# Attention in larger steps: eight transposes at once, value products of 256 queries in two steps beside the sums' reciprocals in one bank

## The chip, the cores and the metric

The kernel runs on one core of a Trainium2 chip. A core has a matrix engine (TensorE, "PE" in the profile; its weight loads are listed apart as "PEld"), a vector engine (VectorE, "DVE"), a scalar engine (ScalarE, "ACT"), a general engine (GpSimd, "POOL") and an engine that issues most transfers (SyncE, "SP"). Each works through its own queue in order, and semaphores tie the queues together. PE writes to PSUM alone, which has eight banks of 128 partitions by 512 float32 numbers; ScalarE and VectorE read them from there.

The metric is the device time of one execution in microseconds, less is better. A measurement is a median over some runs.

## The reference

The model is an encoder trunk of two layers, with 1024 tokens of width 1024 in float32. Layer 0 mixes tokens in two ways side by side: attention with 8 query heads and 2 key heads of width 64, and an RWKV-7 scan of 8 heads in both directions. Layer 1 mixes them with long filters (Hyena). Each layer ends with a SwiGLU network. The change lies in the attention of layer 0 alone:

```python
def one_block(q_blk):
    s = jnp.einsum('bqhgd,bkhd->bhgqk', q_blk, k, preferred_element_type=jnp.float32) * scale
    p = jax.nn.softmax(s, axis=-1)
    return jnp.einsum('bhgqk,bkhd->bqhgd', p.astype(v.dtype), v)
```

Queries go in blocks of 128 against all 1024 keys. The queries and keys were normed and rotated by then.

## The kernel before

**The stage.** `mixer` first streams the input projection (with the first unit's preparation beside it), and then works on the RWKV scan in eight units, one for each pair of heads (`hp`) and direction (`d`). In the loop at the end of `mixer`, turn `i` weaves together what is left of unit `i - 2` (`rwkv_s`: the recurrence over 16 chunks of tokens, one after the other, each a product on PE, then a multiply and add on VectorE at L1500), the products of unit `i - 1` (`rwkv_y`) and the preparation of unit `i` (`rwkv_x`, which ends with a block matrix W that is written to DRAM and read back in another order; L1374 is the first product that needs it). The fourth thread of the weave, `other`, is attention: `beside` goes through `attention` step by step, and when it is through, through `hy_filters`, which prepares the Hyena filters. `weave` takes from its generators in proportion to the steps that each is said to have; a `yield` in a generator is the place where it gives way. The tuple at L1615 says how many steps `other` gets in each turn. The numbers in `beside` (L1607) say after which of attention's steps a piece of the filters' hidden layer is slipped in. The order made so is the program's order; a scheduler that simulates the engines then settles each engine's queue and may move an instruction ahead of others that it takes to be still waiting.

**Attention.** It has 64 score steps: four pairs of heads `t`, eight query blocks `qt`, two heads `e` of the pair. For each,

- `scores` makes 128 queries x 1024 keys in two PSUM banks (L952 and L953, two halves of 512 keys), the maximum of each row on VectorE (L956, L957) and the exponential on ScalarE (L960), which also adds up the row's sum. The result is a page `pr` in SBUF.
- `turn` works on the step before. It turns the 128 x 1024 probabilities over, so that the keys lie on partitions: PE transposes blocks of 128 x 128 (L975, a product with the identity), four into a bank, and ScalarE copies the bank to SBUF (L976). It gives way after each four.
- `values`, after each second query block, multiplies the turned probabilities of 256 queries with the values, for both heads (L996; a float32 product of this kind appears as two matmul records). It gives way after every second of the eight key blocks. Its output stands in the bank `o`, which is taken at `qt` 1 or 5 and kept over two calls until it holds 512 queries. Then the row sums are added up and inverted on VectorE (L1003, L1004), PE spreads them over 64 partitions per head into another bank `rb` (L1008), ScalarE copies them to SBUF (L1010), and VectorE multiplies them with `o` (L1011).

Attention has the four banks of group 1 (`set_banks(4, 4)`), the scan the other four. `bank` takes the bank that has been free longest in the program's order, and `fbank` puts it back at the end of the row; an instruction that reuses a bank waits for the last reader of it.

**Forms of matmul.** The profile names the part of PE's array that a matmul uses. Scores and transposes use 128\*128, value products and the reciprocals' products 128\*64, most products of the scan 64\*64 (L1374, L1430, L1440, L1457, L1499), its preparation 64\*128 (L1310), and a few of its steps 128\*64 (L1421, L1482, L1514) or 128\*128 (L1392).

Of the kernel before, what the change touches and what calls it, by code (L numbers as in the profile page):

```python
# [13 lines left out]
ALU = mybir.AluOpType  # L14
# [7 lines left out]
P = 128  # L22
# [6 lines left out]
H64 = (slice(0, 64), slice(64, 128))  # L29
# [17 lines left out]
def weave(*gens):  # L47


    live = [[0, n, g] for n, g in gens]  # L50
    while live:
        live.sort(key=lambda x: x[0] / x[1])
        s = live[0]
        try:
            cost = next(s[2])
            if cost != "wait":
                s[0] += cost or 1
            elif len(live) > 1:
                s[0] = s[1] * (live[1][0] / live[1][1] + 1e-6)
        except StopIteration:  # L60
            live.pop(0)
# [7 lines left out]
def some(gen, n):  # L69

    for _ in range(n):
        if next(gen, gen) is gen:
            return
        yield


class Kern:
# [834 lines left out]
    def attention(self, out, G):  # L912

        nc = self.nc
        st = {}

        def keys(g):

            kn = self.unspill(self.qd["k"], nc.gpsimd)
            kh, kl = self.page(dt=F32R), self.page(dt=F32R)  # L920
            for X in (g, 1 - g):
                nc.scalar.activation(out=kh[H64[X]], in_=kn[H64[g]], func=AF.Copy)
            for X in (g, 1 - g):
                nc.vector.tensor_tensor(out=kl[H64[X]], in0=kn[H64[g]], in1=kh[H64[g]].bitcast(F32), op=ALU.subtract)
            self.free(kn)
            return kh, kl

        def queries(t):

            q = self.unspill(self.qd[t], nc.gpsimd)  # L930
            qs = [self.page(dt=F32R) for _ in range(2)]
            for e in range(2):
                nc.scalar.activation(out=qs[e][H64[e]], in_=q[H64[e]], func=AF.Copy)
                nc.vector.tensor_tensor(out=qs[e][H64[1 - e]], in0=q[H64[e]], in1=qs[e][H64[e]].bitcast(F32), op=ALU.subtract)
            self.free(q)
            return qs

        def scores(t, qt, e):

            if qt == 0 and e == 0:  # L940
                if t % 2 == 0:
                    if t:
                        self.free(st["k"])
                    st["k"] = keys(t // 2)
                st["qs"] = queries(t)
            if qt % 4 == 0 and e == 0:
                st["s", qt // 4] = self.small("sums", [P, 4, 2, 2], 3)
            kh, kl = st["k"]
            q = st["qs"][e][:, qt * P : (qt + 1) * P]
            ps = [self.bank(G) for _ in range(2)]  # L950
            for n in range(2):
                nc.tensor.matmul(ps[n], q, kh[:, HALVES[n]], start=True, stop=False)  # L952
                nc.tensor.matmul(ps[n], q, kl[:, HALVES[n]], start=False, stop=True)  # L953
            m = self.small("mx", [P, 4], 4)
            for n in range(2):
                nc.vector.tensor_reduce(out=m[:, n : n + 1], in_=ps[n], axis=AX.X, op=ALU.max)  # L956
            nc.vector.tensor_scalar(out=m[:, 2:3], in0=m[:, 0:1], scalar1=m[:, 1:2], scalar2=-0.125, op0=ALU.max, op1=ALU.mult)  # L957
            pr = self.page()
            for n in range(2):
                nc.scalar.activation(out=pr[:, HALVES[n]], in_=ps[n], func=AF.Exp, scale=0.125, bias=m[:, 2:3],  # L960
                                     accum_out=st["s", qt // 4][:, qt % 4, e, n : n + 1])
            self.fbank(ps)
            if qt == 7 and e == 1:
                self.free(st["qs"])
            return pr

        def turn(pr, t, qt, e):

            if qt % 2 == 0:
                st["p", e] = [self.page((P, 4, 256)) for _ in range(2)]  # L970
            for n in range(2):
                pt = self.bank(G, (P, 4, P))
                for j in range(4):
                    k = 4 * n + j
                    nc.tensor.transpose(pt[:, j], pr[:, k * P : (k + 1) * P], self.ident)  # L975
                nc.scalar.copy(st["p", e][n][:, :, P * (qt % 2) : P * (qt % 2) + P], pt)  # L976
                self.fbank(pt)
                yield
            self.free(pr)

        def values(t, qt):

            if "v" not in st:
                st["v"] = self.page((P, 8, P))
                nc.gpsimd.dma_start(out=st["v"].rearrange("p a b -> p (a b)"), in_=self.vd)
            v = st["v"]
            if qt == 1:
                st["y"] = self.page()
            if qt % 4 == 1:
                st["o"] = self.bank(G)  # L990
            o, g = st["o"], t // 2
            x = (qt % 4 - 1) * P
            pT = [st.pop(("p", e)) for e in range(2)]
            for k in range(8):
                for e in range(2):
                    nc.tensor.matmul(o[H64[e], x : x + 256], v[:, k, H64[g]], pT[e][k // 4][:, k % 4], start=k == 0, stop=k == 7)  # L996
                if k % 2 == 1:
                    yield
            self.free(pT)
            if qt % 4 == 3:  # L1000
                s = st.pop(("s", qt // 4))
                rs = self.small("rs", [P, 4, 2], 2)
                nc.vector.tensor_tensor(out=rs, in0=s[:, :, :, 0], in1=s[:, :, :, 1], op=ALU.add)  # L1003
                nc.vector.reciprocal(rs, rs)  # L1004
                rb = self.bank(G, (P, 4, P))
                for j in range(4):
                    for e in range(2):
                        nc.tensor.matmul(rb[H64[e], j], rs[:, j, e : e + 1].to_broadcast([P, 64]), self.ident, start=True, stop=True)  # L1008
                y = st["y"][:, (qt - 3) * P : (qt + 1) * P]
                nc.scalar.copy(y, rb.rearrange("p a b -> p (a b)"))  # L1010
                nc.vector.tensor_tensor(out=y, in0=y, in1=o, op=ALU.mult)  # L1011
                self.fbank(o, rb)
                yield
            if qt == 7:
                out[t] = self.spill(st["y"], f"sp_ya{t}", nc.gpsimd)
                self.free(st["y"])

        steps = [(t, qt, e) for t in range(4) for qt in range(8) for e in range(2)]
        n = len(steps)
        exps = {}  # L1020
        for i in range(n + 1):
            if i < n:
                exps[i] = scores(*steps[i])
                yield
            if i:
                yield from turn(exps.pop(i - 1), *steps[i - 1])
            if i % 4 == 0 and i:
                yield from values(*steps[i - 1][:2])
        self.free(st["k"], st["v"])
# [532 lines left out]
    def mixer(self, w, h, ada, tail):  # L1562
# [18 lines left out]
        out, ys, outr = {}, {}, {}  # L1581
# [21 lines left out]
        def beside():  # L1603
            f = self.hy_filters(1)
            for n, _ in enumerate(att):
                yield
                if n in (208, 228, 248):  # L1607
                    next(f)
            yield from f

        other = beside()
        for i in range(1, len(units) + 2):
            if i == len(units):
                self.free(self.scanm)
            n = (0, 46, 37, 37, 37, 37, 37, 36, 35, 48)[i]  # L1615
            if i > len(units):

                self.fence(F32, 32)
                self.zone = (self.pages, self.beyond)
            gens = [(n, some(other, n))]  # L1620
            if i > 1:
                gens.append((23 if i <= len(units) else 34, self.rwkv_s(units[i - 2], ys, outr, 0)))
            if i <= len(units):
                gens.append((36, self.rwkv_y(units[i - 1], 0)))
            if i < len(units):
                gens.append((16, self.rwkv_x(units[i], 0)))
            weave(*gens)
# [639 lines left out]
```

## Time and profile before

| | us |
|---|---|
| median of 3 runs | 3352.37 |
| lowest and highest | 3352.03, 3354.47 |
| the profiled execution | 3352.85 |
| its span, from the first instruction to the last | 3351.1 |
| the span's mean granted clock of TensorE | 0.961 of full |

The profile is of one execution. Its page gives the busy time of each engine, then the span in 40 equal slices with the busy share of each engine in tenths, then the groups of instructions by source line. Other views of the same trace are used as well. The table by stretches gives busy time and number of instructions of each engine in a window, the granted clock of TensorE, the share of the DMA engines and their rate. The list of waits says for whom an engine stood idle: engine, line, whom it waited for, then the total in us, how often, and the longest one. A row of instruction groups gives busy time and the mean duration in ns behind the bar, then the idle time of the engine just before these instructions and what ended it. A row of the timeline gives the start in us, the duration, the engine, the line, what was done and how many such instructions in a row. The end of a matmul is modelled, and overlaps the next one's start; starts are the safer numbers.

### The profile page before, as it was taken

How to read it: one execution, taken by the hardware profiler on the slowest of the kernel's cores; microseconds unless marked ns; L12 is line 12 of the kernel's file. 1: busy time of each engine (PE TensorE's matmuls, PEld its weight loads, DVE VectorE, ACT ScalarE, POOL GpSimd, SP SyncE). 2: the span in 40 equal slices, each digit the busy share in tenths (PEclk: the TensorE clock that was granted, in tenths of full speed). 3: DMA queues.
4: the chain of work that ended last, by engine and by line, in shares of the span. 5: the costliest groups of instructions: out<-in, count | busy, mean ns of one | idle time of the engine just before them, and what ended most of it. 6: DMA issues, size and time to landing. Idle time of an engine off the chain costs nothing.

```text
span 3351.1 us, 50857 instructions
## 1 busy us (share of the span) xinstructions
PE 3143.0 (94%) x20195; PEld 2552.3 (76%) x20195; DVE 2331.4 (70%) x3755; ACT 1231.4 (37%) x2144; POOL 196.9 (6%) x443
## 2 busy tenths in 40 slices
PE   6999999988989989999999999988977899999998
PEld 4787766766767878888888887877866788888887
DVE  6465565665766897887877666698998686666545
ACT  4632365555546442533333333221220443333211
POOL 2000000000001110000001210000000000000000
PEclk8999999989989999999999999999988999999999
DMA  8654433333323235344448983332446322234311
GB/s 281 219 179 142 142 96 71 74 85 72 100 65 113 85 134 201 101 145 145 157 132 291 353 296 133 107 113 89 145 169 226 132 82 76 76 107 144 118 48 51
DMA packets 331375, 460.23 MB, mean 137 GB/s; under 512 B 101816, under 2 KB 233745, under 8 KB 331136
## 3 DMA queue, kind: packets, MB, share of 16 engines
q1 hardware_dynamic: 292576, 322.04, 31.2%
q0 software_dynamic: 38384, 134.86, 11.4%
q8 instruction: 159, 2.61, 0.3%
q14 instruction: 80, 0.66, 0.1%
q10 hardware_dynamic: 176, 0.07, 0.0%
HBM read 312.71 MB, written 141.56 MB: 136 GB/s over the span
## 4 chain that ended last, share of the span: by engine, by line
PE 73%; DVE 11%; DMA 8%; ACT 3%; issue 3%; SPq 1%; POOL 0%; DVEq 0%; ACTq 0%; POOLq 0%
PE bk L303 27%; PE bk L626 8%; PE bk L628 8%; PE bk L627 8%; PE bk L1840 2%; DVE p L1722 2%; PE bk L1374 2%; PE bk L1310 2%; PE bk L996 1%; PE bk L975 1%; PE bk L1859 1%; DMA p<-in_mix_w_in_dram 1%; DVE p L264 1%; PE bk L952 1%; DMA p<-in_ada_w_dram 1%
## 5 line engine op out<-in xcount | busy, mean ns | idle before, releaser
L303 PE MATMUL bk<-p,p 128*128 128x512 f32 x5136 | 1228.0, 398 | 73.0 <-ACT p L263 43.2
L303 PEld LDWEIGHTS bk<-p,p 128*128 128x128 f32 x5136 | 974.7, 191 | 289.2 <-ACT p L263 45.6
L263 ACT ACTIVATE p<-p 128x512 fp32r<-128x512 f32 (+3 forms) x542 | 403.1, 759 | 937.5 <-PE bk L627 292.3
L264 DVE TENSOR_TENSOR p<-p,p 128x512 fp32r<-128x512 f32 (+3 forms) x542 | 452.1, 850 | 237.4 <-ACT p L263 195.6
L627 PE MATMUL bk<-p,p 128*128 128x512 f32 x1248 | 485.5, 389 | 3.8 <-DVE p L264 3.8
L626 PE MATMUL bk<-p,p 128*128 128x512 f32 x1248 | 485.0, 390 | 0.0
L628 PE MATMUL bk<-p,p 128*128 128x512 f32 x1248 | 484.7, 389 | 0.2 <-DVE p L264 0.2
L627 PEld LDWEIGHTS bk<-p,p 128*128 128x128 f32 x1248 | 234.3, 188 | 53.1 <-DVE p L264 4.7
L628 PEld LDWEIGHTS bk<-p,p 128*128 128x128 f32 x1248 | 234.3, 188 | 49.2 <-DVE p L264 0.6
L626 PEld LDWEIGHTS bk<-p,p 128*128 128x128 f32 x1248 | 234.3, 188 | 48.1
L813 DVE SCALAR_TENSOR_TENSOR p<-bk,mod,p 128x512 f32<-128x512 f32 x192 | 135.0, 746 | 84.7 <-PE bk L303 83.9
L1722 DVE TENSOR_TENSOR p<-p 128x512 f32<-128x512 f32 x240 | 152.9, 692 | 0.4
L455 DVE SCALAR_TENSOR_TENSOR p<-p,cond,p 128x512 f32<-128x512 f32 x140 | 104.6, 749 | 47.7 <-DMA p<-in_ada_w_dram 45.8
L1840 PE MATMUL bk<-p,p 128*128 128x256 f32 x512 | 125.7, 393 | 6.5 <-DVE p L1761 2.3
L956 DVE TENSOR_REDUCE mx<-bk 128x1 f32<-128x512 f32 x128 | 86.6, 686 | 39.1 <-PE bk L953 37.7
L1840 PEld LDWEIGHTS bk<-p,p 128*128 128x128 f32 x512 | 95.1, 193 | 22.4 <-DVE p L1761 3.1
L1068 ACT COPY p<-bk 128x512 f32<-128x512 f32 (+1 forms) x80 | 43.4, 589 | 177.7 <-PE bk L303 70.6
L960 ACT ACTIVATE p<-bk,mx 128x512 f32<-128x512 f32 x128 | 87.2, 688 | 46.4 <-DVE mx L957 42.5
L976 ACT COPY p<-bk 128x512 f32<-128x512 f32 x128 | 73.5, 588 | 77.3 <-PE bk L975 74.6
L1374 PE MATMUL bk<-p,p 64*64 64x64 f32 x2048 | 86.3, 232 | 13.0 <-DMA p<-o 10.4
L1374 PEld LDWEIGHTS bk<-p,p 64*64 64x64 f32 x2048 | 75.4, 144 | 29.2 <-issue 13.5
L975 PE MATMUL bk<-k_ident,p 128*128 128x128 f32 x512 | 88.6, 302 | 8.2 <-ACT p L976 4.7
(408 smaller groups left out, 4134.7 us busy)
## 6 DMA issues: line engine op xcount, KB each, us to landing
p<-in_ffn_w_dram SPq DMA_DIRECT2D x120, 512.0 KB, 4.7
p<-in_ada_w_dram SPq DMA_DIRECT2D x96, 512.0 KB, 4.5
sp_f<-p POOLq DMA_DIRECT2D x36, 512.0 KB, 5.5
p<-sp_f POOLq DMA_DIRECT2D x36, 512.0 KB, 5.8
hs<-p POOLq DMA_DIRECT2D x32, 512.0 KB, 3.1
p<-hs SPq DMA_DIRECT2D x32, 512.0 KB, 4.5
p<-sp_r SPq DMA_DIRECT2D x24, 512.0 KB, 6.3
p<-sp_x SPq DMA_DIRECT2D x24, 512.0 KB, 4.4
```

The costliest lines, as they stand in the source:

```text
L263: self.nc.scalar.activation(out=hi, in_=src, func=AF.Copy)
L264: self.nc.vector.tensor_tensor(out=lo, in0=src, in1=hi.bitcast(F32), op=ALU.subtract)
L303: nc.tensor.matmul(ps[n], a, b[:, HALVES[n]], start=s, stop=e)
L455: nc.vector.scalar_tensor_tensor(out=acc, in0=wt[:, i], scalar=self.cond[:, k : k + 1], in1=acc, op0=ALU.mult, op1=ALU.add)
L626: nc.tensor.matmul(ps, op[:, 0, k], mh, start=start and k == 0, stop=False)
L627: nc.tensor.matmul(ps, op[:, 0, k], ml, start=False, stop=False)
L628: nc.tensor.matmul(ps, op[:, 1, k], mh, start=False, stop=stop and k == 3)
L813: nc.vector.scalar_tensor_tensor(out=xs, in0=ps[n], scalar=self.modc(layer, part, m), in1=xs, op0=ALU.mult, op1=ALU.add)
L975: nc.tensor.transpose(pt[:, j], pr[:, k * P : (k + 1) * P], self.ident)
L1374: nc.tensor.matmul(pt[H[p], pr], lhs(e, pr, p), rhs[H[p], 8 * e + pr], start=True, stop=True)
L1722: tt = lambda o, a, b, op: nc.vector.tensor_tensor(out=o, in0=a, in1=b, op=op)
L1840: nc.tensor.matmul(ps[j][:, ri], F[2 * d + t2 // 4][:, t2 % 4, 128 * ri : 128 * ri + 128], tp[:, j, d], start=d == 0, stop=d == 1)
```

## The change

Four edits, all around `attention`:

- `turn` takes two banks, makes all eight transposes, then both copies, and gives way once.
- `values` gives way once within its eight key blocks, after the fourth, in place of four times.
- `values` takes one bank for each 256 queries and gives it back in the same call: the first half holds the output, the second the spread reciprocals. Sum, reciprocal, spreading, copy and multiplication are thus made for 256 queries each time, 16 times instead of 8. The small tile of reciprocals gets four buffers instead of two. The sums stay in the table `st` until they are written over.
- The shares of attention in the turns of the weave and the places of the filters' pieces are counted in the new, larger steps.

```diff
             if qt % 2 == 0:
                 st["p", e] = [self.page((P, 4, 256)) for _ in range(2)]
+            pts = [self.bank(G, (P, 4, P)) for _ in range(2)]
+            for k in range(8):
+                nc.tensor.transpose(pts[k // 4][:, k % 4], pr[:, k * P : (k + 1) * P], self.ident)
             for n in range(2):
-                pt = self.bank(G, (P, 4, P))
-                for j in range(4):
-                    k = 4 * n + j
-                    nc.tensor.transpose(pt[:, j], pr[:, k * P : (k + 1) * P], self.ident)
-                nc.scalar.copy(st["p", e][n][:, :, P * (qt % 2) : P * (qt % 2) + P], pt)
-                self.fbank(pt)
-                yield
+                nc.scalar.copy(st["p", e][n][:, :, P * (qt % 2) : P * (qt % 2) + P], pts[n])
+            self.fbank(pts)
+            yield
             self.free(pr)
 ...
-            if qt % 4 == 1:
-                st["o"] = self.bank(G)
-            o, g = st["o"], t // 2
-            x = (qt % 4 - 1) * P
+            bank, g = self.bank(G), t // 2
+            o, rb = bank[:, :256], bank[:, 256:]
             pT = [st.pop(("p", e)) for e in range(2)]
             for k in range(8):
                 for e in range(2):
-                    nc.tensor.matmul(o[H64[e], x : x + 256], v[:, k, H64[g]], pT[e][k // 4][:, k % 4], start=k == 0, stop=k == 7)
-                if k % 2 == 1:
+                    nc.tensor.matmul(o[H64[e]], v[:, k, H64[g]], pT[e][k // 4][:, k % 4], start=k == 0, stop=k == 7)
+                if k == 3:
                     yield
             self.free(pT)
-            if qt % 4 == 3:
-                s = st.pop(("s", qt // 4))
-                rs = self.small("rs", [P, 4, 2], 2)
-                nc.vector.tensor_tensor(out=rs, in0=s[:, :, :, 0], in1=s[:, :, :, 1], op=ALU.add)
-                nc.vector.reciprocal(rs, rs)
-                rb = self.bank(G, (P, 4, P))
-                for j in range(4):
-                    for e in range(2):
-                        nc.tensor.matmul(rb[H64[e], j], rs[:, j, e : e + 1].to_broadcast([P, 64]), self.ident, start=True, stop=True)
-                y = st["y"][:, (qt - 3) * P : (qt + 1) * P]
-                nc.scalar.copy(y, rb.rearrange("p a b -> p (a b)"))
-                nc.vector.tensor_tensor(out=y, in0=y, in1=o, op=ALU.mult)
-                self.fbank(o, rb)
-                yield
+            s = st["s", qt // 4]
+            rs = self.small("rs", [P, 2, 2], 4)
+            i = qt % 4 - 1
+            nc.vector.tensor_tensor(out=rs, in0=s[:, i : i + 2, :, 0], in1=s[:, i : i + 2, :, 1], op=ALU.add)
+            nc.vector.reciprocal(rs, rs)
+            for j in range(2):
+                for e in range(2):
+                    nc.tensor.matmul(rb[H64[e], j * P : j * P + P], rs[:, j, e : e + 1].to_broadcast([P, 64]), self.ident, start=True, stop=True)
+            y = st["y"][:, (qt - 1) * P : (qt + 1) * P]
+            nc.scalar.copy(y, rb)
+            nc.vector.tensor_tensor(out=y, in0=y, in1=o, op=ALU.mult)
+            self.fbank(bank)
+            yield
 ...
-                if n in (208, 228, 248):
+                if n in (131, 143, 155):
 ...
-            n = (0, 46, 37, 37, 37, 37, 37, 36, 35, 48)[i]
+            n = (0, 29, 23, 23, 23, 23, 23, 19, 35, 48)[i]
```

## The prediction

> **What bounds the kernel now.** The page comes first: where the time lies, and on which engine.
>
> ```profile
> PE 3143.0 (94%) x20195; PEld 2552.3 (76%) x20195; DVE 2331.4 (70%) x3755; ACT 1231.4 (37%) x2144; POOL 196.9 (6%) x443
> PE   6999999988989989999999999988977899999998
> ```
>
> PE is busy for 94% of the span, so time falls only where PE stops waiting, or does the same work with fewer losses. One slice of the second row is 83.8 us. The attention and RWKV-7 stage that the change touches is a part of slices 6 to 13, where eights stand among nines. The first score product of that stage and its last transposes are these two rows of PE's timeline, and the table by stretches gives what lies between:
>
> ```profile
> 413.44 0.49 PE L952 MATMUL bk<-p,p 128*128 128x512 f32 x1
> ...
> 1027.60 0.96 PE L975 MATMUL bk<-k_ident,p 128*128 128x128 f32 x4
> ```
>
> ```profile
> core 0: us, PE busy (x) PEld busy (x) DVE busy (x) ACT busy (x) POOL busy (x), PEclk, DMA share, GB/s
> 413.00:1040.00 627.00, 569.42 (x7356) 434.13 (x7355) 390.52 (x897) 350.13 (x789) 25.76 (x55) 0.92 0.33 80
> 640.00:720.00 80.00, 70.75 (x955) 55.16 (x954) 51.53 (x115) 43.08 (x93) 3.62 (x6) 0.87 0.43 112
> 800.00:880.00 80.00, 74.16 (x1050) 56.50 (x1044) 50.80 (x122) 46.24 (x102) 3.47 (x7) 0.97 0.40 102
> 1040.00:1120.00 80.00, 78.65 (x829) 65.97 (x828) 62.79 (x108) 36.66 (x72) 9.01 (x17) 1.00 0.36 112
> ```
>
> In the stage's 627 us PE stands still for 627 - 569.4 = 57.6 us, 9%; in the stretch right behind it only for 1.4 of 80. The granted clock is 0.92, against 1.00 behind. VectorE is busy for 62% and ScalarE for 56%. So PE sets the time here, with two kinds of loss: waits, and what it pays between instructions. The waits, longest first:
>
> ```profile
> PE bk L1374 <- DMA p<-o: 10.4, 4, 4.9
> PE bk L952 <- ACT p L960: 7.3, 6, 2.5
> PE bk L1310 <- DVE p L1294: 7.1, 3, 3.5
> PE bk L1392 <- DVE p L1408: 5.1, 4, 2.3
> PE bk L975 <- ACT p L976: 4.7, 5, 2.5
> PE bk L1499 <- DVE p L1500: 4.0, 6, 2.1
> PE bk L975 <- ACT p L960: 3.1, 3, 2.1
> ```
>
> Only the scores (L952) and transposes (L975) in it belong to attention: 15.1 us. The others are the RWKV scan's own chain, for which attention is the filler. The second loss shows in the timeline, where each attention piece stands between pieces of the scan in another form of matmul (128*128 against 64*64). Two rows are of PE's weight loads, the others of PE:
>
> ```profile
> 497.53 0.54 PEld L1457 LDWEIGHTS bk<-p,p 64*64 64x64 f32 x16 [0.17 <-issue]
> 498.73 1.70 PEld L1457 LDWEIGHTS bk<-p,p 64*64 64x64 f32 x54 [0.17 <-issue]
> ```
>
> ```profile
> 497.53 0.68 PE L1457 MATMUL bk<-p,p 64*64 64x64 f32 x16
> 498.14 0.66 PE L975 MATMUL bk<-k_ident,p 128*128 128x128 f32 x4
> 498.73 1.84 PE L1457 MATMUL bk<-p,p 64*64 64x64 f32 x54
> 500.50 1.71 PE L1482 MATMUL bk<-p,p 128*64 128x64 f32 x48
> ...
> 560.50 1.09 PE L975 MATMUL bk<-k_ident,p 128*128 128x128 f32 x8
> ...
> 561.52 0.87 PE L1421 MATMUL bk<-k_ident,p 128*64 128x128 f32 x10
> ```
>
> Read the starts. Four transposes hold PE from 498.14 to 498.73, 0.59 us; eight in one run from 560.50 to 561.52, 1.02 us. Two runs of four are thus 0.16 us dearer than one of eight. The scan pays as well: 54 of its matmuls in one run take 498.73 to 500.50, 32.8 ns each; 16 between two attention pieces take 0.61 us where 16 x 32.8 ns would be 0.52, so 0.09 more. One interruption costs about 0.16 + 0.09 = 0.25 us, if the same form stands on both of its sides. Its weight loads show the same thing as a pause put down to "issue", in which they wait for nobody.
>
> **The change part by part.** The profiled execution took 3352.85 us (span 3351.1 and 1.75 around it); the median of the three runs is 3352.37. The sum is made against the former, which is 0.5 above the median; this is far below my range.
>
> ```profile
> L975 PE MATMUL bk<-k_ident,p 128*128 128x128 f32 x512 | 88.6, 302 | 8.2 <-ACT p L976 4.7 <-ACT p L960 3.1 <-DVE p L1011 0.4
> L996 PE MATMUL bk<-p,p 128*64 128x256 f32 x512 | 74.0, 402 | 1.9 <-ACT p L960 1.8
> L1008 PE MATMUL bk<-k_ident,rs 128*64 128x128 f32 x128 | 10.8, 291 | 0.0
> L1010 ACT COPY p<-bk 128x512 f32<-128x512 f32 x8 | 4.7, 590 | 10.2 <-PE bk L1008 10.2
> L1011 DVE TENSOR_TENSOR p<-p,bk 128x512 f32<-128x512 f32 x8 | 5.5, 681 | 8.5 <-PE bk L996 8.5
> L1003 DVE TENSOR_TENSOR rs<-sums 128x8 f32<-128x8 f32 x8 | 1.3, 160 | 2.8 <-ACT p L960 2.8
> L1004 DVE RECIPROCAL rs<-rs 128x8 f32<-128x8 f32 x8 | 1.6, 199 | 0.1
> L1441 ACT COPY p<-bk 128x256 f32<-128x256 f32 x28 | 10.5, 374 | 13.3 <-PE bk L1440 13.2
> L1465 DVE TENSOR_TENSOR p<-p,bk 128x256 f32<-128x256 f32 x26 | 9.7, 416 | 1.5 <-PE bk L1457 1.3
> ```
>
> *Work.* PE's instructions stay the same in number and shape: 512 transposes, 512 value products, 128 that spread the reciprocals. The 128 copies of transposes stay too. The copy of the reciprocals and the product with it become 16 of 256 columns instead of 8 of 512. By the rows for 256 columns that is 16 x 0.374 - 4.7 = +1.3 us on ScalarE and 16 x 0.416 - 5.5 = +1.2 us on VectorE. Sum and reciprocal are made 16 times for half as many numbers; their time is nearly all fixed, so 8 x 0.36 = +2.9 us on VectorE at most. Both engines are idle for over a third of the stage, so I take 0; uncovered it would be 5.4 us. No DMA is added, removed or moved past a queue.
>
> *Fewer, larger steps (the main term).* Attention gave way to the scan 264 times: 64 after scores, 128 after four transposes each, 64 after value products and 8 after a reciprocal. It now does so 64 + 64 + 32 = 160 times, since the reciprocals' products follow the value products directly, in the same form. That is 104 fewer. The order on PE isn't quite the program's: the 512 transposes run in 121 unbroken runs (95 of exactly four) instead of 128, and scores and transposes together with the value and reciprocal products in 238 instead of 264. So I expect 104 x 238/264 = 94 fewer runs. Where the neighbours are alike, one is worth 0.25 us; where they differ, one change of form remains and half of it, 0.125. Both ends: 94 x 0.125 = 11.8 and 94 x 0.25 = 23.5 us; I take the middle, 17. A part of it falls where PE waits anyhow, 9% of the stage. Term: **-15 us**, between 0 (PE waits instead) and -23.5.
>
> *Banks.* Attention has four PSUM banks. Before, the output bank is held over two value steps, so in half of the steps three are left, and the second four transposes reuse a bank that the exponential of the newest scores still reads. Now nothing is held, and scores and transposes alternate between two pairs. Of the 3.1 us of L975 behind L960 and the 4.7 behind L976, I take **-2 us** (bounds 0 and -7.8), because several of these waits come from a late ScalarE and not from the lack of a bank. Against it, the value bank goes to the next transposes after the copy and the product; that now happens 16 times. The row of L975 has 0.4 us for it in 8 times, so **+1 us**; at worst each waits for both, 16 x (0.374 + 0.416) = 12.6 us. PE's reciprocal products wait for VectorE's reciprocal in the same step. L1008 has 0.0 idle before it today; I take 0, and 16 x 0.36 = 5.8 us at worst. Behind it all of the scan's matmuls would queue.
>
> *Order.* The shares of attention per scan unit (46, 37 ... 36 to 29, 23 ... 19) keep their proportion within one step, except that unit 7 gets about two score steps less. The three pieces of the filters' hidden layer come some 3% later in attention. Both 0, within 4 us either way.
>
> *What is late next.* With 15 us less over seven units, each is 2.1 us shorter. A unit begins with products (L1374) for which a block matrix comes through DRAM, and that latency doesn't shrink. Three handovers show PE waiting for it already (the first row of waits holds all 10.4 us). There the gain is returned, up to 3 x 2.1 = 6.3 us; half, as the first wait also hides behind attention: **+3 us**.
>
> Sum: -15 - 2 + 1 + 3 = -13 us, so 3352.85 - 13 = 3339.9 us: **3340 us**, 0.4% less.
>
> [...] The clock: the two 80 us stretches quoted have 0.87 and 0.97, and PE gets 955 and 1050 instructions done in them, so 0.10 of clock costs 9%. Over the stage 0.02 of clock would cost about 12 us. The eight transposes at 560.50 took 1.09 us, no more than at full pace, so no loss shows in the rows. [...]
>
> **The rivals.**
>
> *The handover sets every unit.* If the scan's own chain through DRAM, and not PE, sets the length of all seven units, the 15 us come back whole: 3352.85 - 2 + 1 = 3352 us. For it: the longest wait is that one. Against it: only three handovers show it, and PE is busy 91%.
>
> *The runs are cut up again.* The order on PE isn't the program's, as here:
>
> ```profile
> 1029.45 0.50 PE L1514 MATMUL bk<-p,p 128*64 128x64 f32 x9
> 1029.74 0.32 PE L1008 MATMUL bk<-k_ident,rs 128*64 128x128 f32 x1
> 1029.79 0.22 PE L1514 MATMUL bk<-p,p 128*64 128x64 f32 x1
> ```
>
> Then the change doesn't do what it says, and only the banks count: 3352 us. Against it: 95 of 121 runs are exactly the program's four.
>
> *The state chain loses its cover (slower).* The scan's recurrence goes PE (L1499), VectorE (L1500), PE, link by link, and what stands between links is attention in small pieces:
>
> ```profile
> L1500 DVE SCALAR_TENSOR_TENSOR p<-bk,DC,p 128x64 f32<-128x64 f32 x84 | 23.5, 280 | 45.3 <-PE bk L1499 43.6 <-PE bk L1430 1.4
> 877.07 0.33 PE L1499 MATMUL bk<-p,p 64*64 64x64 f32 x4 [0.39 <-DVE p L1500]
> ...
> 878.51 0.48 PE L1499 MATMUL bk<-p,p 64*64 64x64 f32 x4 [0.39 <-DVE p L1500]
> ```
>
> A link without cover stalls PE for 0.39 us. There are 84, so 33 us if all were bare; 4.0 us are paid now. With fewer pieces more links follow each other directly. It decides from 13/0.39 = 33 further bare links, 40% of them; with 60%, 3352.85 - 13 + 50 x 0.39 = 3359 us. Against it: per link there remain more than one attention piece and two or three scan pieces.
>
> **How the numbers follow.** Forecast (3322 to 3346): 0.62. Handover 0.13 and cut runs 0.08, both within 0.2% (6.7 us, about what a measurement of this kernel can tell from no change). State chain 0.14, and the clock 0.03 (0.03 less, 18 us against the 13: 3358 us): slower. So faster 0.62, same 0.21, slower 0.17. The low end is full price for each run and all of L975's bank waits, -23.5 - 7.8 + 1 = -30: 3322. The high end takes in both neutral rivals and the nearer half of the slower ones: 3360.
>
> **What would show it.** Right: about 60 runs of transposes, most of eight; some 30 runs of value and reciprocal products; more PE instructions per us in the stage at an unchanged count; the stage shorter by about 13 us, all else as before. The bank term: L975 behind L960 nearly gone. Wrong: L1374 behind its DMA over 15 us (handover), L1499 behind L1500 over 15 us (state chain), L1008 behind L1004 at all, or a granted clock below 0.92.

## The result, and the profile after

| | us |
|---|---|
| before, median of 4 runs (lowest, highest) | 3353.42 (3352.03, 3355.23) |
| after, median of 4 runs (lowest, highest) | 3330.93 (3327.18, 3339.04) |
| ratio after to before, with its 95% interval | 0.9938 [0.9923, 0.9953] |
| profiled execution of after, its span | 3339.04, 3337.3 |

The change takes 22.5 us off by the medians, 16 to 26 by the interval. The forecast was 3340 us and the range 3322 to 3360. The profiled execution of after is the slowest of its four runs. So the two traces lie 13.8 us apart where the medians lie 22.5 apart, and a reading of the traces can explain only the former. That is the first thing to keep in mind below: single runs of one kernel differ. In the first series of experiments the kernel before had 35 runs, and they went from 3338.72 to 3363.89 us.

The page of after, engine busy times and PE's row of slices:

```profile
PE 3131.2 (94%) x20195; PEld 2554.8 (77%) x20195; DVE 2331.1 (70%) x3779; ACT 1229.3 (37%) x2152; POOL 197.5 (6%) x443
PE   6999999988899989999999999988977999999998
```

PE's busy time fell by 11.8 us at the same 20195 instructions. Between these two traces the gain is thus mostly work that PE does with fewer losses, and little of it is waiting less. To see where, cut the stage at two points that both kernels have: the first score product, and the first product of the eighth and last unit's recurrence (L1482, after it L1478), which comes after all of attention. Units are counted from 1 here. In code that follows the edits, line numbers of after are lower by 4 (L1374 is now L1370, L1499 is L1495). The transposes are L973, their copies L975, the value products L993, the multiplication with the reciprocals L1007. The table by stretches, before:

```profile
core 0: us, PE busy (x) PEld busy (x) DVE busy (x) ACT busy (x) POOL busy (x), PEclk, DMA share, GB/s
413.40:1146.80 733.40, 674.47 (x8619) 522.67 (x8618) 475.18 (x1043) 402.11 (x896) 39.96 (x81) 0.93 0.33 84
413.40:950.50 537.10, 491.73 (x6463) 374.06 (x6462) 335.16 (x774) 298.12 (x682) 19.44 (x43) 0.93 0.35 85
950.50:1062.50 112.00, 99.78 (x1141) 78.43 (x1141) 67.67 (x147) 63.87 (x127) 7.38 (x14) 0.86 0.28 74
```

and after:

```profile
core 0: us, PE busy (x) PEld busy (x) DVE busy (x) ACT busy (x) POOL busy (x), PEclk, DMA share, GB/s
414.60:1132.80 718.20, 655.47 (x8619) 517.37 (x8618) 474.01 (x1066) 402.27 (x902) 40.33 (x80) 0.94 0.34 86
414.60:955.40 540.80, 489.02 (x6474) 379.11 (x6473) 341.29 (x808) 307.82 (x708) 19.91 (x43) 0.93 0.35 85
955.40:1049.20 93.80, 84.26 (x1138) 68.56 (x1136) 60.37 (x135) 55.62 (x109) 7.28 (x13) 0.93 0.32 83
```

The whole stage (first row of each) went from 733.4 to 718.2 us with the same 8619 matmuls. PE's busy time in it fell by 19.0, and its idle time rose from 58.9 to 62.7. The other two rows go up to the first L1374 (L1370 after) of unit 7, and from there to the first one of unit 8. The six units ahead are 3.7 us longer than before; more of attention lies in them, 1271 of its matmuls instead of 1248. Unit 7, which has 136 of them instead of 160, is 18.2 us shorter. So the whole gain of the stage stands in the one unit whose share was cut, though the larger steps are in all units. In the six ahead, 59 changes of form fewer (432 for 491) stand against 6.4 us more idle time. The 18.2 us of unit 7 are not all less work: its granted clock is 0.93 instead of 0.86. PE's waits in the stage, after:

```profile
PE bk L1370 <- DMA p<-o: 11.5, 6, 3.7
PE bk L952 <- ACT p L960: 9.4, 7, 4.1
PE bk L1811 <- DVE p L1774: 6.6, 2, 3.7
PE bk L1495 <- DVE p L1496: 4.9, 6, 1.4
PE bk L973 <- ACT p L975: 4.5, 4, 1.8
PE bk L973 <- DVE p L1007: 4.5, 3, 1.8
...
PE bk L993 <- ACT p L960: 1.9, 4, 0.7
```

The transposes no longer wait for the exponential (3.1 us before). In its place stand a wait for the multiplication that frees the value bank (L973 behind L1007, 4.5 us) and longer ones behind the exponential, at the scores and the values. The groups of the edited part:

```profile
L973 PE MATMUL bk<-k_ident,p 128*128 128x128 f32 x512 | 81.7, 290 | 9.2 <-ACT p L975 4.5 <-DVE p L1007 4.5
L993 PE MATMUL bk<-p,p 128*64 128x256 f32 x512 | 69.1, 406 | 2.0 <-ACT p L960 1.9
L1004 PE MATMUL bk<-k_ident,rs 128*64 128x128 f32 x128 | 13.0, 275 | 0.0
L1007 DVE TENSOR_TENSOR p<-p,bk 128x256 f32<-128x256 f32 x16 | 6.7, 418 | 27.3 <-ACT p L1006 27.3
L1001 DVE RECIPROCAL rs<-rs 128x4 f32<-128x4 f32 x16 | 2.8, 175 | 0.3
```

Three pieces of PE's timeline show how a step now runs:

```profile
568.26 1.09 PE L973 MATMUL bk<-k_ident,p 128*128 128x128 f32 x8
...
578.06 1.95 PE L993 MATMUL bk<-p,p 128*64 128x256 f32 x16
579.83 0.61 PE L1004 MATMUL bk<-k_ident,rs 128*64 128x128 f32 x8
...
585.20 0.66 PE L973 MATMUL bk<-k_ident,p 128*128 128x128 f32 x4
586.99 0.66 PE L973 MATMUL bk<-k_ident,p 128*128 128x128 f32 x4 [1.13 <-DVE p L1007]
```

The first is the intended step of eight. In the second the reciprocals' products follow the value products with no pause. In the third the eight come in two halves with nothing between them but a wait: the second bank isn't free yet, since the multiplication still reads it, and PE stands for 1.13 us.

### The profile page after: what moved, and what is told of

Same layout as the page of the kernel before. It is cut to its first block, busy times and chain, and to the rows that moved or that the text cites. A ratio compares the mean times of both kernels' runs of the same rounds, so it can differ in the third digit from the quotient of the medians.

```text
span 3337.3 us, 50889 instructions
## 1 busy us (share of the span) xinstructions
PE 3131.2 (94%) x20195; PEld 2554.8 (77%) x20195; DVE 2331.1 (70%) x3779; ACT 1229.3 (37%) x2152; POOL 197.5 (6%) x443
## 3 DMA queue, kind: packets, MB, share of 16 engines
q0 software_dynamic: 38384, 134.86, 11.6%
## 4 chain that ended last, share of the span: by engine, by line
PE 73%; DVE 10%; DMA 8%; ACT 3%; issue 3%; SPq 1%; POOL 0%; DVEq 0%; ACTq 0%; POOLq 0%
PE bk L303 27%; PE bk L626 8%; PE bk L627 8%; PE bk L628 8%; PE bk L1836 3%; PE bk L1855 2%; DVE p L1718 2%; PE bk L1370 1%; PE bk L1306 1%; PE bk L973 1%; DMA p<-in_mix_w_in_dram 1%; PE bk L1811 1%; PE bk L993 1%; DMA p<-in_ada_w_dram 1%; PE bk L952 1%
## 5 line engine op out<-in xcount | busy, mean ns | idle before, releaser
L504 ACT ACTIVATE p<-p 128x512 f32<-128x512 f32 x80 | 49.9, 632 | 138.0 <-DVE p L840 114.5
L1370 PE MATMUL bk<-p,p 64*64 64x64 f32 x2048 | 82.9, 227 | 13.1 <-DMA p<-o 11.5
L975 ACT COPY p<-bk 128x512 f32<-128x512 f32 x128 | 73.1, 589 | 54.9 <-PE bk L973 49.6
L1370 PEld LDWEIGHTS bk<-p,p 64*64 64x64 f32 x2048 | 72.0, 139 | 26.6 <-DMA p<-o 13.0
```

Of the source, the lines that this page charges most:

```text
L1370: nc.tensor.matmul(pt[H[p], pr], lhs(e, pr, p), rhs[H[p], 8 * e + pr], start=True, stop=True)
```

## The experiments

Two theories stood at the start. **A:** fewer changes between forms of matmul on PE, which the larger steps bring, make the gain. **B:** the shares per unit, or just the one order that came out, make it. The experiments separate shares, banks and steps, disturb the order by a single step without touching the work, and go further in the direction of the change.

| kernel | median us (runs) | ratio to before, 95% |
|---|---|---|
| e1: before with the change's shares | 3345.67 (12) | 0.9983 [0.9969, 0.9997] |
| e2: the change with before's shares | 3346.24 (12) | 0.9981 [0.9967, 0.9994] |
| e3: one bank alone, small steps | 3354.99 (12) | 1.0010 [0.9996, 1.0024] |
| e4: large steps alone, old banks | 3348.93 (12) | 0.9990 [0.9976, 1.0004] |
| e5: the change again | 3332.82 (6) | 0.9933 [0.9918, 0.9948] |
| e6: the change, shares moved by one step | 3352.51 (12) | 1.0005 [0.9991, 1.0019] |
| e7: before, shares moved by one step | 3361.21 (12) | 1.0021 [1.0007, 1.0034] |
| e8: scores and transposes in one step too | 3347.34 (11) | 0.9984 [0.9972, 0.9997] |
| e9: the change, shares moved the other way | 3344.88 (11) | 0.9974 [0.9960, 0.9988] |
| e10: the change, filter pieces one step earlier | 3338.45 (10) | 0.9967 [0.9954, 0.9981] |
| e11: before, shares moved the other way | 3350.89 (12) | 0.9999 [0.9981, 1.0017] |
| e12: before, filter pieces earlier | 3346.70 (12) | 0.9987 [0.9975, 0.9998] |

The kernel before gave medians of 3352.71, 3352.38 and 3353.42 in the three series (e1 to e4, e5 to e8, e9 to e12), and each ratio is to the one of its own series.

**Shares apart from steps.** e1 is the kernel before with each unit's attention as the change has it, counted in the old small steps; e2 is the change with the old proportions.

```diff
 e1, against before
-                if n in (208, 228, 248):
+                if n in (217, 237, 257):
-            n = (0, 46, 37, 37, 37, 37, 37, 36, 35, 48)[i]
+            n = (0, 49, 38, 38, 38, 38, 38, 28, 35, 48)[i]
 e2, against after
-                if n in (131, 143, 155):
+                if n in (125, 137, 150):
-            n = (0, 29, 23, 23, 23, 23, 23, 19, 35, 48)[i]
+            n = (0, 27, 23, 22, 22, 23, 22, 24, 35, 48)[i]
```

> The kernel before with its fine steps and its old banks; only the shares of attention per scan unit and the places of the filter pieces are those of the change, scaled from 160 to 264 steps (49, 38, 38, 38, 38, 38, 28 and 217, 237, 257). Shares theory (the gain came in the last unit because two score steps of attention and the filter pieces were moved): about 10 us faster than before, 0.997. Form theory (the gain is the fewer changes of matmul form on TensorE; the built order has 552 of them here, 563 before, 473 after the change, so 22.5 us for 90 is 0.25 us each): 11 x 0.25 = 3 us faster, 0.999.

> The changed kernel, but with the shares and places of before scaled from 264 to 160 steps (27, 23, 22, 22, 23, 22, 24 and 125, 137, 150). Shares theory: half of the gain is lost, 0.997. Form theory: 479 changes of form in the built order against 473 of the change and 563 of before, so 84 x 0.25 = 21 us faster than before, 0.9937.

Each gives about 6 us, together some 12 of the 22. Neither alone is the change. e1 lies between its two forecasts. e2 agrees with the 0.997 of the shares theory, and is far from the 0.9937 that 0.25 us per change of form gave for it, although it has the change's number of them within one (554). The runs below show besides that 6 us is no more than an order alone can be worth, so these two can't be put down to shares or steps. e2 also shows the slower rival of the prediction, in its list of waits:

```profile
PE bk L952 <- ACT p L960: 16.8, 14, 2.4
PE bk L1495 <- DVE p L1496: 16.7, 8, 7.1
```

With the shares spread so, PE stands 16.7 us in the recurrence's chain, and 16.8 behind the exponential. The larger steps can take the cover away; in the change itself they did not (4.9 us).

**Bank apart from steps.** e3 has the new bank use in `values`, but gives way as often as before; e4 has the new steps with the old banks, its output bank again held over two calls.

```diff
 e3: values as in after, but
-                if k == 3:
+                if k % 2 == 1:
                     yield
 (turn as before; shares 51, 39 ... 39, 29; pieces 224, 244, 265)
 e4: turn as in after; values as before, but
-                if k % 2 == 1:
+                if k == 3:
                     yield
 ...
-                yield
+            yield
 (shares and pieces as after)
```

> Only the bank is changed: output and reciprocals of 256 queries in one bank that is given back at once; transposes by four and value products by two key blocks as before, 272 steps, the shares of the change scaled to them. Step theory, as predicted (the larger steps are the main term, the banks 1 us): about 1 us faster, 0.9997. Form theory: the built order has 502 changes of form, because the free bank lets transposes follow each other; 61 x 0.25 = 15 us faster, 0.9955.

> Only the steps are larger: eight transposes at once, value products in two steps, but one output bank held over two calls and another for the reciprocals of 512 queries, as before. Step theory, as predicted: 12 to 15 us faster, 0.996. Form theory: 521 changes of form in the built order, 42 x 0.25 = 10 us faster, 0.997; the two differ little in time here, and the number of attention runs tells: 144 by the step theory, 212 in the built order.

Alone neither differs from before beyond its interval. Neither theory got e4. For e3 the 0.9997 of the step theory holds, and the 15 us that the form theory gave were far off. In the traces attention stands in 203 runs on PE in e3 and 219 in e4, after 238 before; the large steps alone thus did little to join them. e3's waits show what stands against its fewer runs:

```profile
PE bk L952 <- ACT p L960: 26.4, 13, 4.0
...
PE bk L975 <- DVE p L1008: 6.4, 4, 2.7
```

(In e3 the transposes are L975, and L1008 is the multiplication that frees the bank.) The scores stand 26.4 us behind the exponential, against 7.3 before: attention seems to come to its turn more quickly than ScalarE is done. The parts don't add up to the whole: 3.4 - 3.4 = 0 us from e3 and e4, where the change gives 22. Something else than a sum of parts was at work, and the next runs look for it.

**The same work in another order.** e5 is the change once more. In e6 and e7 the shares are moved by a step from unit to unit, in e9 and e11 the other way; in e10 and e12 only the filters' pieces come a little earlier. No instruction is added or taken away.

```diff
 e6, e9, against after
-            n = (0, 29, 23, 23, 23, 23, 23, 19, 35, 48)[i]
+            n = (0, 30, 22, 24, 22, 24, 22, 19, 35, 48)[i]   e6
+            n = (0, 28, 24, 22, 24, 22, 24, 19, 35, 48)[i]   e9
 e7, e11, against before
-            n = (0, 46, 37, 37, 37, 37, 37, 36, 35, 48)[i]
+            n = (0, 47, 36, 38, 36, 38, 36, 36, 35, 48)[i]   e7
+            n = (0, 45, 38, 36, 38, 36, 38, 36, 35, 48)[i]   e11
 e10, against after
-                if n in (131, 143, 155):
+                if n in (130, 142, 154):
 e12, against before
-                if n in (208, 228, 248):
+                if n in (205, 225, 245):
```

> The changed kernel once more, in as many runs as the experiments have, since single runs of one kernel have spread over 12 to 25 us. If its gain is its own: 3330 us, 0.9935. If the first four runs were lucky: as its neighbours of the first experiments, 0.997 to 0.998.

> The changed kernel with shares moved by one step to and fro between the units (30, 22, 24, 22, 24, 22, 19), which gives no unit more than one step more or less than the change does. Theory of the steps (large steps and a free bank bring the gain, whatever the exact order): 0.994, within 5 us of the change. Theory of the draw (each small edit makes the scheduler settle another order, and the orders differ by 5 to 10 us in how the waits fall): anywhere between 0.993 and 0.999.

> The kernel before with its shares moved by one step to and fro (47, 36, 38, 36, 38, 36, 36). Theory of the steps: no change, 1.000 within 0.001. Theory of the draw: a change of 5 to 10 us either way, 0.997 to 1.003.

> The changed kernel with shares moved by one step the other way (28, 24, 22, 24, 22, 24, 19). By the ten stages seen so far, the time in which TensorE works fits 513 us + 0.36 per us at half clock + 0.20 per change of form within 3 us. The built order has 470 changes of form, as few as the change (473), so its part of the gain, 16 us, stays; waits and half clock fall anew. Theory of the draw: 0.993 to 1.000, and the distance to the change (0.9933) shows as half clock and idle time in one or two units, not as more changes of form. Theory of the steps alone: 0.993 to 0.995.

> The changed kernel with the three pieces of the filters' hidden layer one step earlier (130, 142, 154), nothing else. Theory of the draw: 0.993 to 1.000, and another one than in the run above. Theory that the place of the pieces decides (the 24 us at half clock in the jolted change began where its first piece stood): clearly off 0.9933, with the difference in units 6 and 7 only.

> The kernel before with its shares moved by one step the other way (45, 38, 36, 38, 36, 38, 36); 565 changes of form in the built order, 563 before. Theory of the draw: 0.998 to 1.003; the four kernels with the old steps then lie about 1.000, and those with the new steps some 0.003 to 0.005 below it on average.

> The kernel before with the three pieces of the filters' hidden layer three fine steps earlier (205, 225, 245), nothing else. Theory of the draw: 0.998 to 1.003. If the places of the pieces decide: off 1.000 by 5 us or more, with the difference after the first piece, at about 890 us, only.

e5 repeats the result (0.9933 against 0.9938), so it belongs to this kernel and not to one occasion. But shares moved by one step take all of it away (e6: 1.0005), and the other neighbours keep about a half or less (0.9967, 0.9974). Neighbours of the kernel before spread as well, from 0.9987 to 1.0021. The order alone is worth some ±0.3% here, nearly as much as the 0.4% that the change was forecast to bring. All neighbours but e6, which is beyond the 0.999 named for it, fall where the theory of the draw put them. In e10 the place of a piece is a part of it: up to the first product of unit 6 its stage takes 454.3 us, 458.6 in after and 457.3 in e5, and units 6 and 7, where the pieces stand, take 185.7 us for 176.0 and 172.8, with 22.9 us of idle PE for 15.2 and 13.4. In e12 the like move gave 4 us, less than the 5 named as its sign.

Where e6 loses it, its trace shows. Up to the end of unit 4 it is ahead of after. Units 5 and 6 (cut at the first L1370 of each) then take 193.3 us in e6 and 171.3 in after. The tables by stretches, e6 first:

```profile
777.90:971.20 193.30, 171.45 (x2118) 131.09 (x2119) 112.71 (x267) 99.02 (x222) 6.02 (x12) 0.84 0.30 67
900.00:924.00 24.00, 24.00 (x136) 15.61 (x136) 13.18 (x25) 9.77 (x19) 0.44 (x2) 0.51 0.00 1
```

```profile
784.10:955.40 171.30, 156.73 (x2155) 121.35 (x2155) 115.59 (x277) 99.88 (x227) 6.65 (x14) 0.93 0.35 86
900.00:924.00 24.00, 23.02 (x326) 18.18 (x322) 15.77 (x37) 15.23 (x34) 0.89 (x2) 1.00 0.09 14
```

Of the 22 us, PE's idle time is 7.3 (21.9 against 14.6). Half clock is probably the larger part: by the records of the granted clock it lasts 61 us of e6's two units and 24 of after's, which at the 0.35 us found below makes 13. The second rows show the worst of it. In e6 PE is granted half the clock for 24 us, though it is shown busy all the time, and starts 136 matmuls where after starts 326 at full clock. The timeline of e6 has a wait of PE 10 us ahead of it, a run of eight transposes within it, and a link of the recurrence that waits behind it:

```profile
889.99 1.98 PE L1306 MATMUL bk<-p,p 64*128 64x128 f32 x16 [3.65 <-DVE p L1289]
...
914.10 1.97 PE L973 MATMUL bk<-k_ident,p 128*128 128x128 f32 x8
916.00 0.48 PE L1370 MATMUL bk<-p,p 64*64 64x64 f32 x4
...
947.77 0.48 PE L1495 MATMUL bk<-p,p 64*64 64x64 f32 x4 [5.24 <-DVE p L1496]
```

The eight take 1.90 us from start to start, where 568.26 in after has 1.02. The profiled run of e6 took 3361.99 us, 9.5 more than its median, so not each run has all of this. Half-clock stretches in this stage of the traces last 3.4, 6.8, 10.2 or 13.7 us, and 23.9 here. What keeps the clock down for 24 us is not shown: PE's row is busy in 24.00 of 24.00. Busy is modelled from the instructions' ends, so PE may have been less active than it says.

**Further in the same direction.** e8 gives way after a whole score step with its transposes, and only twice at the start between them.

```diff
 e8, against after
-                yield
+                if i < 2:
+                    yield
 ...
-                if n in (131, 143, 155):
+                if n in (79, 87, 94):
-            n = (0, 29, 23, 23, 23, 23, 23, 19, 35, 48)[i]
+            n = (0, 17, 14, 14, 14, 14, 14, 14, 35, 48)[i]
```

> The changed kernel, with scores and the transposes of the step before made in one step, without giving way between them: both are of the 128x128 form. 98 steps instead of 160, shares scaled. Theory of the steps with a price per change of form: the built order has 413 changes, 60 fewer than the change; at 0.15 to 0.25 us each 9 to 15 us faster than the change, 0.990. If the pieces are by now too large to cover the scan's own chain: slower than the change, 0.996 or more, with more idle time of the state products and of the scores behind the exponential.

Fewer changes of form did come (501 in the stage, after 553), and PE's busy time fell by 4 us against after, but not the time:

```profile
413.30:1139.80 726.50, 651.15 (x8621) 523.47 (x8620) 475.55 (x1066) 405.49 (x907) 41.17 (x78) 0.93 0.33 85
```

```profile
PE bk L952 <- ACT p L960: 23.5, 11, 3.7
PE bk L1371 <- DMA p<-o: 6.6, 3, 3.5
PE bk L973 <- DVE p L1007: 6.0, 6, 1.7
```

(L1371 is the handover of W here.) The scores meet the exponential again, for 23.5 us, as the second of the two forecasts said; the state products, named with them there, do not (4.1 us). No tried version beats the change.

**One sum for all kernels.** For each of the 14 profiles I read the stage, PE's idle time in it, the time for which the records of the granted clock give half and the number of places where one matmul on PE is followed by one of another form. Each row is one execution, which in e1, e6 and e7 took some 10 us more than the kernel's median.

| | stage us | PE idle us | half clock us | changes of form |
|---|---|---|---|---|
| before | 733.4 | 58.9 | 105.8 | 635 |
| e1 | 725.6 | 56.6 | 75.1 | 636 |
| e7 | 744.6 | 63.3 | 126.3 | 612 |
| e11 | 730.6 | 60.6 | 78.5 | 637 |
| e12 | 724.0 | 55.5 | 88.7 | 626 |
| e3 | 730.2 | 70.0 | 99.0 | 581 |
| e4 | 727.4 | 57.7 | 92.2 | 605 |
| after | 718.2 | 62.7 | 85.3 | 553 |
| e5 | 713.6 | 60.6 | 81.9 | 553 |
| e2 | 720.2 | 73.6 | 68.3 | 554 |
| e6 | 740.3 | 67.0 | 122.9 | 572 |
| e9 | 720.1 | 66.3 | 88.7 | 552 |
| e10 | 723.6 | 67.1 | 81.9 | 553 |
| e8 | 726.4 | 75.3 | 105.8 | 501 |

A straight-line fit gives stage - idle = 515.5 + 0.35 x half clock + 0.198 x changes (all in us; the two factors to ±0.04 and ±0.017), and no kernel lies over 4.5 us off it. By the fit a change of form thus costs 0.20 us of PE's busy time, and a microsecond at half clock 0.35. Attention's runs in place of the changes fit a little worse (5.1 us at most), and beside them add nothing clear.

The traces also give the price directly, and it is lower. Take the matmuls at full clock that wait for nothing, and read from start to start: when the next one has another form it comes 0.12 to 0.13 us later, in the mean of each of the 14 profiles (418 to 512 changes in each), than when the same instruction is repeated; another line of the same form costs under 0.02 us. That is the 0.125 us of the prediction. So the fit's 0.20 isn't all spent at the changes. Nor is busy time the whole stage: kernels with fewer changes have more idle time. Fitted to the stage instead of stage - idle, the same two columns give 0.39 for half clock and only 0.08 us per change (±0.03).

From before to after the fit gives -82 x 0.198 = -16.2 us for changes, -20.5 x 0.35 = -7.2 for the clock, and +3.8 of idle: -19.6 where -15.2 were measured in the two traces. The difference, 4.4, is what the fit leaves over. By the direct price the 82 changes are 82 x 0.12 = 10 us, and by the fit of the stage 82 x 0.08 = 7 us is what is left of them once the new waits are counted.

## Why the prediction was right, and what was not

**The bound and the mechanism** were right as far as they go: in this stage PE sets the time (busy for 655.5 of 718.2 us), and fewer changes of form (553 for 635, at 0.12 us each by the rows) take busy time off it. But e6, e9 and e10 have the change's number of them within 20 and not its gain, so the mechanism is a part of the 22.5 us and not the whole. The stage became 15.2 us shorter, and the rest of the span 1.4 longer.

**Fewer, larger steps: -15 us predicted.** By the fit the size came out, -16.2, by two errors that cancel; by the direct price it was too large, -10. I expected 94 fewer runs of attention on PE at 0.18 us. There were 64 fewer, 238 before and 174 after, since the transposes stand in 106 runs (62 of four and only 23 of eight among them), not about 60. Of the 64 steps 41 are cut, 24 of the 44 cuts with scores between the parts, the others with pieces of the scan alone. Most cuts, 34, fall after the fourth transpose, where the second bank begins; that a bank not yet free, as at 585.20, lets the scheduler put other work there is likely, but not shown. Value and reciprocal products stand in 36 runs (64 before), near the 30 expected. A third of the rival "the runs are cut up again" thus happened. But what costs is the change of form, on whichever side of a run it stands, and of those 82 went, at 0.12 us each by the rows and 0.20 by the fit.

**Banks: -2 us, and +1 for the value bank.** The removed wait was there: the transposes waited for the exponential for 5.4 us on average in the five profiles with the old steps (before, e1, e7, e11, e12), for 0.3 in the five with the new ones (e5, e2, e6, e9, e10; all of it in e2). But it came back elsewhere, by the same averages: transposes behind the multiplication that frees the value bank 0.6 to 4.1 us, values behind the exponential 2.2 to 4.2, scores behind it 8.7 to 12.4, the state chain 4.8 to 7.5 (by e2's 16.7 alone). PE's idle time in all rose from 59 to 67. Where I had +2 for banks and handover together, the waits gave some 8 us back. A bank that is free earlier didn't free PE; that attention which comes sooner meets ScalarE sooner fits all of this, e3's 26.4 us most plainly.

**Handover of W: +3 us.** L1370 behind its DMA is 11.5 us for 10.4, and 11.6 for 10.1 in the averages. The rival that it sets every unit is out: in the five profiles with the new steps it is 8.6 to 13.6 us, below the 15 that were named as its sign. (e1, with the old steps, has 16.2 and is not slower, so the sign was a weak one.)

**The state chain** (slower): 4.9 us for 4.0, so not in the change; e2's 16.7 us shows that it was a real possibility, decided by the shares.

**The reciprocal's wait** was 0, and L1004 has 0.0 idle. **The clock:** the stage was granted 0.94, before 0.93, and a run of eight transposes at 568.26 took 1.02 us, as long as the one at 560.50 before. That the larger steps lower the clock, for which the prediction has 0.03, no run shows: half clock lasts 68 to 123 us in the six profiles of the change and its four relatives, 75 to 126 in the five of before and its four, and in e8, with the largest steps, as long as in before (105.8). The prediction's price was somewhat high: 0.02 of clock is 25 us of half clock in 627, which at 0.35 makes 9 us and not 12.

**Order and shares: "0, within 4 us either way".** This is the step that failed. The forecast 3340 lies 9 us above the measured time, and the other terms, with 10 to 16 us of changes and the waits that came back, don't account for it. The kernel before with the new shares lies 6 us below it (e1), and moving single steps moves the time of either kernel by more than 4: by the ratios, the change's neighbours lie 11 to 24 us above e5 (e10, e9, e6), those of before 4 us below to 7 above the kernel before (e12, e7). What then belongs to the change? Mean ratio of before and its four relatives: 0.9998. Mean of the change and its four: 0.9972, 9 us less. Without before and the change themselves, four against four: 0.99975 and 0.9982, 5 us less, with a standard error of about 4 (a ratio of 0.0016, under the 0.003 to 0.005 expected with e11). So the larger steps as such are worth some 5 to 9 us; the 7 us that the fit of the stage leaves to the changes agree, but at that error it is likely rather than shown. The remaining 14 to 17 us of the 22.5 came with this one order, and that was luck. Theory A thus holds for the smaller part of the gain, and theory B, as one order among others, for the larger. Against the means of its four relatives, the two profiles of the change (after, e5) have 7 us less idle time and 7 us less half clock (2.4 us by the price above), so about 9 us of it can be named. Which accident of order keeps the exponential and the handover out of PE's way in just this one is not settled.

Without the luck of the order the same steps would have come to some 3344 to 3348 us, above the forecast instead of below it.

## What to carry to other kernels

Where one engine weaves several streams of work, count the changes of form at its queue, price one by the starts of neighbouring runs in the timeline, and look at what the woven engine waits for next: here 10 to 16 us of changes came with some 8 of new waits. Before a gain of 0.3% is put down to an edit, move one step of the order without changing the work and see what that is worth. An edit that changes step sizes changes the order too, and the two can be told apart only by several orders of each.

## What was not expected of the hardware

In e6 half clock lasts 24 us in one stretch, with PE shown busy throughout. Four of the eight 33\*64 products of the filters' hidden layer fall mostly into it, but these products stand in each of the other kernels as well, where no stretch of the stage is over 13.7 us. Over all kernels half clock is 68 to 126 us of a stage of some 725, and this spread alone is worth 0.35 x 58 = 20 us, as much as the change. A change of form between matmuls costs 0.12 to 0.13 us at full clock, from start to start, and this is the same in all 14 profiles; from 128\*128 to 64\*64 it is 0.09 us, the other way round 0.13 to 0.15. Why the fit over whole kernels makes it 0.20, and what holds the clock down for so long, stays open.
